# A two-layer trunk on one core: output tiles in the order of tokens' later experts, each step an iteration behind the last, and the last three experts' tokens from rows on chip

## The chip, the cores and the metric

The kernel runs on one core of a Trainium2 chip. The metric is device time in microseconds of one execution; the kernel before is given as the median of three runs. Engine names: PE is TensorE, DVE VectorE, ACT ScalarE, POOL GpSimd, SP SyncE (here only a DMA queue). "L933" is line 933 of the kernel before.

## The reference

A trunk of two layers over 1024 tokens with 16 meta tokens prepended (1040 rows of 1024 numbers). Layer 0 mixes by causal pooling, layer 1 by latent attention; each ends with a mixture of experts, added to the residual. A final root-mean-square norm gives the output, without the meta rows.

```
h = concat(meta_tokens, x)                          # (1040, 1024)
h = h + pool_mixer(rmsnorm(h)); h = h + moe(rmsnorm(h), layer 0)
k, v = shared_latent_kv(h)
h = h + mla_mixer(rmsnorm(h), k, v); h = h + moe(rmsnorm(h), layer 1)
return rmsnorm(h, final_norm)[:, 16:]

def moe(h):                     # 4 groups of 8 experts, D_EXPERT = 256
    g_sel = argmax(softmax(h @ wr_g + br_g)); w_g = max of it
    top_v, top_i = top_k(logits of the group's 8 experts, 2)
    gate = w_g * softmax(top_v)
    for each token and each of its two experts e:
        out[token] += gate * ((silu(x @ w_gate[e]) * (x @ w_up[e])) @ w_down[e])
```

So each token's result is its residual row plus two weighted expert rows, and both of its experts lie in one group of eight.

## The kernel before

Layer 0 runs to about 441 us of the profiled span, the latents and attention to about 975, layer 1's mixture of experts from about 980, the rest of the output after it.

**Routing.** For every token the router (class with `order`, `place_ids`, `lists`) finds its two experts, its rank among the tokens of each, and from these the tables `gi` (which row of h_d each of an expert's up to CAP = 96 places takes), `di` (which row of y_d the result goes to) and the gates. y_d has two halves of L = 1040 rows, one for the first and one for the second expert of a token; h_d holds the residual rows with the normed input. Tokens beyond 96 of an expert go through `overflow` behind the loop, under a branch that does not run with these inputs.

**The expert loop, `Moe.run`.** Iteration e of 33 does, in program order: the gather `ga(e+3)` on GpSimd's DMA queue (L839, 96 rows into one of NX = 6 buffers `xg`); `out.begin(e)`; the down products of expert e-1 and the up products of e on TensorE (L1378 to L1380, three products for each piece split into a high and a low part by ScalarE, L1373, and VectorE, L1374); the transposes of e+1 and their scaling (L860); `rows`, L933, on VectorE, which weighs expert e-1's result and adds the row it was gathered from; `scatter`, L845, 96 rows to y_d; the split of the next x; `out.middle(e)`; the second halves of the products; Silu on ScalarE (L908) and its product on VectorE (L909); `out.end(e)`. The order on every engine is the order of the program. Weights stream through a ring of 17 slots of 1 MB, issued on SP (L827), three a iteration, each waiting for its slot.

**Output under the loop, class `Out`.** Before the change the tokens are put in the order of their expert group: `order` (end of iteration 3) works out each token's place, `place_ids` (L798) writes 128 token numbers to list_d by an indirect DMA, one tile an iteration in iterations 4 to 11, `load_list` (L804) reads the list back on SP in iteration 12, and `lists` makes the row indices. Then `EARLY_OUT` gives tile t an iteration a: in begin(a) both rows of each of its 128 tokens are fetched from y_d (`fetch`, L1097, two gathers of 512 KB), in end(a) VectorE adds them (L1111) and ScalarE squares (L1112), in middle(a+1) VectorE finds the root (L1109, L174 to L184), in end(a+1) it multiplies (L1114), in begin(a+2) the tile is stored (`store`, L1102). Five tiles go this way, in iterations 17, 20, 25, 27 and 29, all through one pair of buffers; `rest` does the other three after the loop, planned by `Sched`. `again`, under a branch, repeats the five if the group order did not suit them.

In dependence tracking an indirect DMA that writes a tensor waits for the one before that wrote it, unless `declare_no_dep` says otherwise; the scatters to y_d are declared apart from one another, the writes of `place_ids` are not. A fetch of y_d waits for the scatters before it, and a scatter behind a fetch waits for the fetch.

## Time and profile before

| | us |
|---|---|
| median of three runs | 1407.7 |
| the runs | 1407.33, 1407.7, 1410.6 |
| the profiled execution's own time | 1410.51 |
| its span | 1408.3 |
| mean granted TensorE clock | 0.954 of full |
| TensorE busy | 1267.9 (90% of the span) |
| VectorE busy | 1054.2 (75%) |
| ScalarE busy | 746.2 (53%) |
| GpSimd busy | 341.4 (24%) |

The median is over whole executions; the profile is of one. The span leaves out 2.2 us of that execution's own time. Busy shares are over the whole span, so they mix stages with different limits.

### The profile page before, as it was taken

The numbers are of one execution on the slowest core, as the hardware profiler recorded it, in microseconds if no ns is written. First come the engines' busy times: TensorE is split into PE (matmuls) and PEld (weight loads), VectorE is DVE, ScalarE is ACT, GpSimd is POOL, SyncE is SP. The second block draws the span as 40 slices with busy tenths as digits, with TensorE's granted clock in tenths as the row PEclk, the third lists the DMA queues.
The fourth block names the chain that finished last, engine by engine and source line by source line (L and its number), as shares of the span: only waits on it lengthen the run. The fifth ranks groups of instructions, "written<-read, shape, count | busy, mean of one in ns | idle before, by whom it ended". The sixth has DMA issues, their size and how long they took to land. (4 is left out here: it accounts for less than half of the span.)

```text
span 1408.3 us, 22733 instructions
## 1 busy us (share of the span) xinstructions
PE 1267.9 (90%) x8027; PEld 1093.4 (78%) x8027; DVE 1054.2 (75%) x2507; ACT 746.2 (53%) x1591; POOL 341.4 (24%) x469
## 2 busy tenths in 40 slices
PE   7979999999995999999999999996999996696870
PEld 5977888888884998989888899985888885585650
DVE  5777888888887676676776777688788885595863
ACT  4445655565655455655655665554556563354440
POOL 0122222222211441232221223213133222122312
PEclk9989999999998999999999999997999998898995
DMA  8927999999945303320010010467899999897213
...
DMA packets 80314, 293.48 MB, mean 208 GB/s; under 512 B 21409, under 2 KB 28833, under 8 KB 63682
## 3 DMA queue, kind: packets, MB, share of 16 engines
...
q8 instruction: 65, 1.06, 0.3%
...
## 5 line engine op out<-in xcount | busy, mean ns | idle before, releaser
L1378 PE MATMUL py<-wp,hT 128*96 128x512 f32 x256 | 115.8, 452 | 43.9 <-ACT hT L1373 43.9
L1378 PE MATMUL gu<-wp,xT 128*96 128x256 f32 x512 | 147.3, 288 | 0.0
L1380 PE MATMUL gu<-wp,xT 128*96 128x256 f32 x512 | 143.4, 280 | 0.0
L1379 PE MATMUL gu<-wp,xT 128*96 128x256 f32 x512 | 143.3, 280 | 0.0
L1374 DVE TENSOR_TENSOR wp<-slotB,wp 128x512 fp32r<-128x512 f32 x160 | 107.0, 690 | 22.5 <-ACT wp L1373 21.6
L1373 ACT ACTIVATE wp<-slotB 128x512 fp32r<-128x512 f32 x160 | 96.0, 626 | 23.8 <-PE py L1380 20.2
L1380 PE MATMUL py<-wp,hT 128*96 128x512 f32 x256 | 104.9, 410 | 1.0 <-DVE hT L1374 0.4
L1379 PE MATMUL py<-wp,hT 128*96 128x512 f32 x256 | 103.7, 405 | 0.0
L2281 POOL TENSOR_TENSOR hh<-hh,wt 128x512 f32<-128x512 f32 x56 | 72.3, 1291 | 111.2 <-ACT wt L2280 109.1
L845 POOL DMA_INDIRECT y_d<-xg,di x34 | 34.2, 1006 | 246.9 <-DVE xg L933 210.7
L1373 ACT ACTIVATE xT<-xq 128x384 fp32r<-128x384 f32 x64 | 33.6, 526 | 111.1 <-DVE xq L860 111.1
L1378 PEld LDWEIGHTS py<-wp,hT 128*96 128x96 f32 x256 | 43.2, 169 | 62.2 <-ACT hT L1373 46.4
L1378 PEld LDWEIGHTS gu<-wp,xT 128*96 128x96 f32 x512 | 84.8, 166 | 0.1
L1380 PEld LDWEIGHTS gu<-wp,xT 128*96 128x96 f32 x512 | 83.1, 162 | 0.0
L1379 PEld LDWEIGHTS gu<-wp,xT 128*96 128x96 f32 x512 | 82.9, 162 | 0.1
L884 PE MATMUL gu<-slotB,xq 128*96 128x256 f32 x320 | 75.6, 379 | 0.0
L2117 ACT ACTIVATE P<-bank,sm 128x400 f32<-128x400 f32 (+3 forms) x112 | 59.6, 540 | 25.7 <-DVE sm L2107 25.5
L1870 DVE TENSOR_TENSOR T<-bank,T 128x512 fp32r<-128x512 f32 (+2 forms) x112 | 53.7, 496 | 20.7 <-ACT T L1866 19.7
L860 DVE TENSOR_TENSOR xq<-pt,ffg 128x768 f32<-128x768 f32 (+1 forms) x66 | 61.0, 927 | 8.1 <-PE pt L857 8.1
L2284 DVE SCALAR_TENSOR_TENSOR hh<-bank,ri,hh 128x512 f32<-128x512 f32 x72 | 53.6, 747 | 15.8 <-PE bank L1380 15.4
L1374 DVE TENSOR_TENSOR wp<-slotR,wp 128x512 fp32r<-128x512 f32 x80 | 53.2, 690 | 13.9 <-ACT wp L1373 13.6
L1374 DVE TENSOR_TENSOR wp<-hh,wp 128x512 fp32r<-128x512 f32 x82 | 54.8, 690 | 11.4 <-ACT wp L1373 10.9
...
## 6 DMA issues: line engine op xcount, KB each, us to landing
...
hh<-w_up SPq DMA_DIRECT2D x10, 1024.0 KB, 10.9
...
```

The lines of the kernel that those rows point to most:

```text
L845: return nc.gpsimd.indirect_dma_start(out=self.r.y_d, out_offset=bass.IndirectOffsetOnAxis(ap=didx, axis=0), in_=y[:CAP], in_offset=None, ...
L860: nc.vector.tensor_tensor(x[:, 4 * a:4 * (a + w)].rearrange("p (a b) c -> p a b c", a=w), pt[:, a:a + w].rearrange("p a (b c) -> p a b c", ...
L884: nc.tensor.matmul(gu[:CAP, f * FE:f * FE + FE], lhsT=x[0][:, j], rhs=w[:, j], start=(f == 0 and j == 0), stop=False)
L1373: nc.scalar.activation(dH, src, AF.Copy)
L1374: nc.vector.tensor_tensor(dL, src, dH.bitcast(F32), op=OP.subtract)
L1378: nc.tensor.matmul(out, lhsT=aH, rhs=bH, start=start, stop=False)
L1379: nc.tensor.matmul(out, lhsT=aH, rhs=bL, start=False, stop=False)
L1380: nc.tensor.matmul(out, lhsT=aL, rhs=bH, start=False, stop=stop)
L1870: nc.vector.tensor_tensor(dL, src, dH.bitcast(F32), op=OP.subtract)
L2117: nc.scalar.activation(self.P[hd, qp][a][:, x0:x0 + xe], tt[:, :xe], AF.Exp, bias=sm[:, 3:4], scale=SCALE, accum_out=sm[:, x:x + 1])
L2281: done(end), s.op("G", end + s.LAT, 1170, lambda: nc.gpsimd.tensor_tensor(k.h[i][:, cs], k.h[i][:, cs], x, op=OP.add), lambda end: s.relea ...
L2284: s.op("V", now + s.LAT, 70 + 1.04 * 512, lambda: nc.vector.scalar_tensor_tensor(k.h[i][:, cs], p, self.ri[hd, i], k.h[i][:, cs], op0=OP.m ...
```

## The change

Tokens are ordered by their later expert (the larger number of the two) instead of by group. `Out` takes over the working; `EARLY_OUT` is now the list of iterations (9, 13, 17, 21, 25, 29, 30) in which seven tiles are fetched.

- The ordering (`order`) is six small steps: `later` in end(0), `masks` in end(1), a pair of matmuls `sums` in begin(2), `starts` in end(2), `places` in end(3), `suits` in end(4). Two operations a batch in the router and one in the counts, which served the group order, go.
- `place_ids` is called four times in begin(4) and four times in begin(5); `load_list` in begin(6); `lists` in end(8). `load_tokens` (begin 6 to 8) gathers the token numbers of the last three experts, `tokens` (end 10) makes indices of them.
- A loaded tile's steps are an iteration apart each: fetch in begin(f); add on GpSimd in begin(f+1), square on ScalarE in middle(f+1), root on VectorE in end(f+1); gain (by the final norm's row) on GpSimd in begin(f+2), scale on ScalarE in middle(f+2); store in begin(f+3). Before, add and gain were VectorE's.
- Tiles 5 and 6 end around the last iterations, and the tokens whose later expert is 29, 30 or 31 (DIRECT = 3) take that expert's rows from the `xg` buffer on chip and fetch only the row of the other expert (`other`). Their store goes by `keep`. `rest` is called inside iteration 32 around the last scatter.
- Fetches and scatters are declared apart from one another (`out.got`), and so are stores.
- In layer 1 the overflow branch stands ahead of the loop, in both layers its room is `xg[5]` instead of `xg[1]`; `again` does all eight tiles through plain loads.
- CLEAR goes from 20000 to 30000, between pieces of the clearing of y_d in the middle stage.

```diff
-EARLY_OUT = ((0, 17, 256), (1, 20, 256), (2, 25, 640), (3, 27, 640), (4, 29, 640))
-LIST_AT = 3
-CLEAR = 20000
-FINAL_START = 2000
+EARLY_OUT = (9, 13, 17, 21, 25, 29, 30)
+DIRECT = 3
+CLEAR = 30000
...
+    def order(self, psum, c):
+        k, V, n = self.k, self.k.nc.vector, len(self.tiles)
+        m = c[1][:, :n * NE].rearrange("p (n e) -> p n e", n=n)
+        q = c[0][:, :n * NE].rearrange("p (n e) -> p n e", n=n)
+        cum = [c[0][:, 512 + NE * i:512 + NE * i + NE] for i in range(2)]
+        st, p, b = c[0][:, 640:640 + NE], c[0][:, 704:704 + n], c[0][:, 720:729]
+        w, tot = c[0][:, :2 * n * NE], c[0][:, 672:672 + NE]
+        pr = psum.tile([128, 2, NE], F32, name="pr", tag="pr", bufs=1)
+        def later():
+            V.tensor_tensor(w.rearrange("p (n e) -> p n e", e=NE), self.oh.rearrange("p n j e -> p (n j) e"),
+                            k.iota32.unsqueeze(1).to_broadcast([128, 2 * n, NE]), op=OP.mult)
+            V.tensor_reduce(self.later.unsqueeze(2), w.rearrange("p (n x) -> p n x", n=n), axis=AX.X, op=OP.max)
+        def masks():
+            V.tensor_tensor(m, k.iota32.unsqueeze(1).to_broadcast([128, n, NE]),
+                            self.later.unsqueeze(2).to_broadcast([128, n, NE]), op=OP.is_equal)
+            V.tensor_reduce(c[0][:, 736:736 + NE].unsqueeze(2), m.rearrange("p n e -> p e n"), axis=AX.X, op=OP.add)
+            V.tensor_copy(self.cnt, c[0][:, 736:736 + NE])
+            V.scalar_tensor_tensor(self.ids, self.v[:, :, 0, 0], float(BIG), self.v[:, :, 0, 1], op0=OP.add, op1=OP.add)
+            V.scalar_tensor_tensor(self.later, self.later, float(BIG), self.ids, op0=OP.mult, op1=OP.add)
+            with k.nc.allow_non_contiguous_dma("one number a row"):
+                for i, t, x in self.runs():
+                    k.nc.sync.dma_start(out=self.later_d[t * 128:(t + x) * 128].rearrange("(t p) o -> p (t o)", p=128),
+                                        in_=self.later[:, i:i + x])
+        def sums():
+            k.nc.tensor.matmul(pr[:, 0], lhsT=k.tri, rhs=self.cnt, start=True, stop=True)
+            k.nc.tensor.matmul(pr[:, 1], lhsT=k.ones, rhs=self.cnt, start=True, stop=True)
+        def starts():
+            a = tot
+            V.tensor_copy(tot, pr[:, 1])
+            for i, n2 in enumerate((1, 2, 4, 8, 16)):
+                x = cum[i % 2]
+                V.tensor_copy(x[:, :n2], a[:, :n2])
+                V.tensor_tensor(x[:, n2:], a[:, n2:], a[:, :NE - n2], op=OP.add)
+                a = x
+            V.tensor_tensor(st, a, tot, op=OP.subtract)
+            V.tensor_tensor(q[:, 0], st, pr[:, 0], op=OP.add)
+        def places():
+            for i in range(n - 1):
+                V.tensor_tensor(q[:, i + 1], q[:, i], m[:, i], op=OP.add)
+            V.tensor_tensor(q, q, m, op=OP.mult)
+            V.tensor_reduce(p.unsqueeze(2), q, axis=AX.X, op=OP.add)
+            V.tensor_copy(self.place, p)
+        def suits():
+            t = len(EARLY_OUT)
+            lim, pos = c[0][:, 768:768 + t], c[0][:, 784:784 + t]
+            for i, e in enumerate(EARLY_OUT):
+                V.tensor_copy(lim[:, i:i + 1], st[:, e - 1:e])
+            V.scalar_tensor_tensor(pos, k.iota32[:, :t], 128.0, self.v[:, 0, 0, 1:2].to_broadcast([128, t]), op0=OP.mult, op1=OP.add)
+            V.tensor_tensor(self.past, pos, lim, op=OP.is_ge)
+            V.scalar_tensor_tensor(b[:, :t - 1], k.iota32[:, 1:t], 128.0, lim[:, :t - 1], op0=OP.mult, op1=OP.is_gt)
+            V.tensor_scalar(b[:, t - 1:t], lim[:, t - 1:], float(128 * t), None, op0=OP.is_gt)
+            V.tensor_reduce(b[:, t:t + 1].unsqueeze(2), self.ex[:, NE - DIRECT:].unsqueeze(1), axis=AX.X, op=OP.add)
+            V.tensor_reduce(b[:, 8:9].unsqueeze(2), b[:, :t + 1].unsqueeze(1), axis=AX.X, op=OP.add)
+            V.tensor_copy(self.bad, b[:, 8:9])
+        return later, masks, sums, starts, places, suits
...
+        V, ids = self.k.nc.vector, self.ids[:, :len(EARLY_OUT)]
+        V.scalar_tensor_tensor(ids, self.past, float(BIG), ids, op0=OP.mult, op1=OP.add)
+        V.tensor_scalar(ids, ids, float(S), None, op0=OP.min)
         for j in range(2):
-            self.k.nc.vector.tensor_scalar(self.list[:, j], self.ids, float(j * L), None, op0=OP.add)
+            V.tensor_scalar(self.list[:, j], self.ids, float(j * L), None, op0=OP.add)
+    def load_tokens(self, i):
+        e = NE - DIRECT + i
+        if i == 0:
+            self.k.nc.vector.memset(self.token, float(NE * BIG))
+        self.k.nc.gpsimd.indirect_dma_start(
+            out=self.token[:CAP, i:i + 1], out_offset=None, in_=self.later_d,
+            in_offset=bass.IndirectOffsetOnAxis(ap=self.gi[:CAP, e:e + 1], axis=0), bounds_check=S - 1, oob_is_err=False)
+    def tokens(self):
+        V = self.k.nc.vector
+        V.scalar_tensor_tensor(self.token, self.k.iota32[:, NE - DIRECT:], -float(BIG), self.token, op0=OP.mult, op1=OP.add)
+        V.tensor_copy(self.ti[:CAP, 0], self.token[:CAP])
+        V.scalar_tensor_tensor(self.token[:CAP], self.token[:CAP], 2.0, self.of[:CAP], op0=OP.mult, op1=OP.subtract)
+        V.tensor_scalar(self.ti[:CAP, 1], self.token[:CAP], float(L), None, op0=OP.add)
...
-            for o in self.scat:
+            for o in self.scat + (out.got if out else []):
...
+        if out:
+            self.overflow(nx, scatter, True)
...
+                if out and e == NE:
+                    out.last()
                 self.rows(ps, r.table[:CAP, 0, e - 1:e], y)
-                scatter(y, r.di[:CAP, e - 1:e])
+                put = lambda y=y, e=e: scatter(y, r.di[:CAP, e - 1:e])
+                if out and e == NE:
+                    out.rest(put)
+                else:
+                    put()
...
-        room = [k.xg[1], 0]
+        room = [k.xg[NX - 1], 0]
+        xg = k.xg[NX - 2]
...
+    def apart(self, x, others):
+        for o in others:
+            self.k.tc.declare_no_dep(x.ins, o.ins, reason="other tokens' rows")
 
     def fetch(self, t, c):
         for j in range(2):
-            self.k.nc.gpsimd.indirect_dma_start(
+            x = self.k.nc.gpsimd.indirect_dma_start(
                 out=c[j], out_offset=None, in_=self.r.y_d, in_offset=bass.IndirectOffsetOnAxis(ap=self.r.list[:, j, t:t + 1], axis=0),
-                bounds_check=2 * L - 1, oob_is_err=True)
+                bounds_check=2 * L - 1, oob_is_err=False)
+            self.got.append(x)
 
     def store(self, t, c):
...
+        self.keep(c, self.r.list[:, 0, t:t + 1])
+    def keep(self, c, ids):
+        n = ids.shape[0]
+        x = self.k.nc.gpsimd.indirect_dma_start(
+            out=self.out[0], out_offset=bass.IndirectOffsetOnAxis(ap=ids, axis=0), in_=c[0][:n], in_offset=None,
+            bounds_check=S - 1, oob_is_err=False)
+        self.apart(x, self.put)
+        self.put.append(x)
+    def other(self, i, o):
+        x = self.k.nc.gpsimd.indirect_dma_start(
+            out=o[:CAP], out_offset=None, in_=self.r.y_d, in_offset=bass.IndirectOffsetOnAxis(ap=self.r.ti[:CAP, 1, i:i + 1], axis=0),
+            bounds_check=2 * L - 1, oob_is_err=False)
+        self.got.append(x)
+    def add(self, eng, c, n=128):
+        eng.tensor_tensor(c[0][:n], c[0][:n], c[1][:n], op=OP.add)
+    def square(self, c, i, n=128):
+        self.k.nc.scalar.activation(c[-1].bitcast(BF16)[:n, :D], c[0][:n], AF.Square, accum_out=self.st[:n, 0, i:i + 1])
+    def root(self, i, n=1):
+        st = self.st[:, :, i:i + n]
+        self.k.nc.vector.tensor_scalar(st[:, 1], st[:, 0], 1.0 / D, EPS, op0=OP.mult, op1=OP.add)
+        for f in rsqrt_ops(self.k, st[:, 2], st[:, 1], st[:, 3]):
+            f()
+    def gain(self, c, n=128):
+        self.k.nc.gpsimd.tensor_tensor(c[0][:n], c[0][:n], self.g[:n], op=OP.mult)
+    def scale(self, c, i, n=128):
+        self.k.nc.scalar.activation(c[0][:n], c[0][:n], AF.Copy, scale=self.st[:n, 2, i:i + 1])
+    def both(self, c, i, n=128):
+        self.k.nc.vector.scalar_tensor_tensor(c[0][:n], c[0][:n], self.st[:n, 2, i:i + 1], self.g[:n], op0=OP.mult, op1=OP.mult)
+    def rows(self, i):
+        x = self.k.xg
+        free = x[(NE - DIRECT) % NX]
+        return [(x[(NE - 4) % NX], self.a[1], self.b[1])[i], x[(NE - DIRECT + i) % NX], self.b[1] if i == 0 else free]
 
 
     def begin(self, e):
-        r = self.r
+        k, r, nc = self.k, self.r, self.k.nc
+        later, masks, sums, starts, places, suits = self.order
+        if e == 2:
+            sums()
         for i in range(len(r.tiles)):
-            if e == LIST_AT + 1 + i:
+            if e == 4 + i // 4:
                 r.place_ids(i)
-        if e == LIST_AT + 1 + len(r.tiles):
+        if e == 6:
             r.load_list()
...
+        if 5 < e < 6 + DIRECT:
+            r.load_tokens(e - 6)
+        for t, f in enumerate(EARLY_OUT[:-2]):
+            if e == f:
+                self.fetch(t, self.a)
+            if e == f + 1:
+                self.add(nc.gpsimd, self.a)
+            if e == f + 2:
+                self.gain(self.a)
+            if e == f + 3:
+                self.store(t, self.a)
+        if e == NE - 3:
+            self.fetch(5, self.a)
+        if e == NE - 2:
+            self.add(nc.gpsimd, self.a)
+            self.fetch(6, self.b)
+            self.other(0, self.rows(0)[0])
+        if e == NE - 1:
+            self.add(nc.gpsimd, self.b)
+            self.add(nc.gpsimd, self.rows(0), CAP)
+            self.other(1, self.rows(1)[0])
+            self.gain(self.a)
+        if e == NE:
+            self.add(nc.gpsimd, self.rows(1), CAP)
+            self.other(2, self.rows(2)[0])
 
     def middle(self, e):
 
-        for t, a, _ in EARLY_OUT:
-            if e == a + 1:
-                for _, _, f in self.steps(self.c, self.st)[2:-1]:
-                    f()
+        for f in EARLY_OUT[:-2]:
+            if e == f + 1:
+                self.square(self.a, 0)
+            if e == f + 2:
+                self.scale(self.a, 0)
+        if e == NE - 2:
+            self.square(self.a, 0)
+        if e == NE - 1:
+            self.square(self.b, 1)
+            self.square(self.rows(0), 2, CAP)
 
     def end(self, e):
...
+        k, r = self.k, self.r
+        later, masks, sums, starts, places, suits = self.order
+        if e == 0:
+            k.nc.vector.memset(self.st, 1.0)
+            k.nc.sync.dma_start(out=self.g, in_=bcast_row(k.A["final_norm"], D))
+            later()
+        if e == 1:
+            masks()
+        if e == 2:
+            starts()
+        if e == 3:
+            places()
+        if e == 4:
+            suits()
+        if e == 8:
             r.lists()
...
+        if e == 10:
+            r.tokens()
+        for f in EARLY_OUT[:-1]:
+            if e == f + 1:
+                self.root(0)
+    def last(self):
+        self.scale(self.a, 0)
+        self.square(self.rows(1), 3, CAP)
+        self.root(1, 3)
+    def rest(self, scatter):
+        nc, V, r = self.k.nc, self.k.nc.vector, self.r
+        b, d = self.b, [self.rows(i) for i in range(DIRECT)]
+        self.store(5, self.a)
+        self.gain(b)
+        scatter()
+        self.gain(d[0], CAP)
+        self.add(V, d[2], CAP)
+        self.scale(b, 1)
+        self.square(d[2], 4, CAP)
+        self.scale(d[0], 2, CAP)
+        self.both(d[1], 3, CAP)
+        self.root(4)
+        self.both(d[2], 4, CAP)
+        self.store(6, b)
+        for i in (1, 0, 2):
+            self.keep(d[i], r.ti[:CAP, 0, i:i + 1])
...
-        self.s.op("Q", now, 0, lambda: self.clear(0, now))
+        self.s.op("Q", now + CLEAR, 0, lambda: self.clear(0, now + CLEAR))
```

## Rows read from the trace of the kernel before

**Rows 1.** Busy time by stretch: length, engines (instructions), granted clock, DMA share, GB/s
```profile
1002.00:1154.00 152.00, 151.60 (x931) 125.89 (x930) 131.09 (x212) 89.85 (x166) 41.94 (x38) 1.00 0.98 328
1154.00:1284.00 130.00, 101.10 (x591) 81.15 (x589) 86.91 (x141) 56.49 (x105) 30.19 (x26) 0.91 0.93 344
1284.00:1370.00 86.00, 67.10 (x360) 50.78 (x360) 63.39 (x111) 40.52 (x76) 20.36 (x17) 0.90 0.31 104
```

**Rows 2.** Waits by engine, 1000 to 1371: total us, times, longest
```profile
DVE out L1111 <- DMA out<-y_d,list: 37.5, 5, 11.4
```

**Rows 3.** Timeline of VectorE in the loop: start, us, instruction [idle before]
```profile
1001.93 1.27 DVE L933 SCALAR_TENSOR_TENSOR xg<-py,table,xg 96x1024 f32<-96x1024 f32 x1
...
1154.15 1.27 DVE L933 SCALAR_TENSOR_TENSOR xgh<-py,table,xgh 96x1024 f32<-96x1024 f32 x1
...
1164.23 1.27 DVE L933 SCALAR_TENSOR_TENSOR hh<-py,table,hh 96x1024 f32<-96x1024 f32 x1
...
1176.96 1.23 DVE L1111 TENSOR_TENSOR out<-out,out 128x1024 f32<-128x1024 f32 x1 [10.20 <-DMA out<-y_d,list]
...
1183.03 0.69 DVE L1374 TENSOR_TENSOR wp<-slotR,wp 128x512 fp32r<-128x512 f32 x1 [0.30 <-ACT wp L1373]
...
1188.21 1.27 DVE L933 SCALAR_TENSOR_TENSOR hh<-py,table,hh 96x1024 f32<-96x1024 f32 x1
...
1189.87 0.14 DVE L1109 TENSOR_SCALAR ost<-ost 128x1 f32<-128x1 f32 x1
...
1191.39 0.16 DVE L184 SCALAR_TENSOR_TENSOR ost<-ost 128x1 f32<-128x1 f32 x1
...
1352.98 1.27 DVE L933 SCALAR_TENSOR_TENSOR hh<-py,table,hh 96x1024 f32<-96x1024 f32 x1
```

**Rows 4.** Timeline behind the loop, all engines
```profile
1370.07 1.28 DVE L933 SCALAR_TENSOR_TENSOR xg<-py,table,xg 96x1024 f32<-96x1024 f32 x1 [1.45 <-PE py L1380]
1371.62 0.91 POOL L845 DMA_INDIRECT y_d<-xg,di  x1 [5.88 <-DVE xg L933]
...
1376.11 1.05 POOL L1097 DMA_INDIRECT c<-y_d,list  x1 [3.58 <-DVE xg L1023]
...
1384.33 1.06 ACT L1112 ACTIVATE c<-c 128x1024 bf16<-128x1024 f32 x1 [16.66 <-DVE c L1111]
...
1399.52 0.96 POOL L1102 DMA_INDIRECT out<-c,list  x1 [3.12 <-issue]
```

**Rows 5.** Timeline at the end of layer 0, all engines
```profile
441.30 0.06 DVE L1023 MEMSET xg<- 128x1 f32 x1 [3.98 <-DMA y_d<-xg,di]
...
442.05 3.28 ACT L1433 ACTIVATE wH<-slotA,gk 128x320 fp32r<-128x320 f32 x7 [8.41 <-DVEq L1029]
```

**Rows 6.** Timeline of GpSimd and VectorE, 478 to 482
```profile
478.57 2.39 POOL L1828 TENSOR_TENSOR hh<-hh,qr 128x1024 f32<-128x1024 f32 x1
...
479.34 1.63 DVE L182 TENSOR_TENSOR st<-st 128x2 f32<-128x2 f32 x1
```

**Rows 7.** Line L798, the writes of the list
```profile
  DMA list_d<-ids,place: 9.7, 6
...
DMA to landing us min/median/max: 8.8/10.1/11.5
```

**Rows 8.** DMA issues of 1000 to 1160: count, KB, median us to landing
```profile
y_d<-xg,di POOLq DMA_INDIRECT x9, 8.4
xg<-h_d,gi POOLq DMA_INDIRECT x9, 10.9
...
ids<-list_d SPq DMA_DIRECT2D x1, 4.0 KB, 25.1
```

**Rows 9.** DMA issues of 1287 to 1409
```profile
y_d<-xg,di POOLq DMA_INDIRECT x5, 3.6
out<-y_d,list POOLq DMA_INDIRECT x4, 4.8
```

**Rows 10.** Timeline of GpSimd in iteration 17, 1160 to 1200
```profile
1164.30 1.05 POOL L1097 DMA_INDIRECT out<-y_d,list  x1 [6.04 <-DMA y_d<-xgh,di]
```

249 lines of the change are left out of this document (101 added, 148 removed).

## The prediction

> **What bounds the kernel now.** I read the busy time of stretches first [rows 1]. From 1002 to 1154 us TensorE is busy for 151.6 of 152 us at full clock: the expert loop runs at TensorE's pace. From 1154 to 1284 it is busy for 101.1 of 130, from 1284 to 1370 for 67.1 of 86. So what this change can win lies in some 48 us of holes in the loop and in the 38.3 us from 1370 to the span's end at 1408.3. It cannot win in the first stretch, only lose there.
>
> The waits name the holes [rows 2]: five adds of output tiles on VectorE waited 37.5 us in all for the fetch of rows of y_d. The VectorE rows show what one costs [rows 3]. An undisturbed iteration takes 10.08 us (1154.15 to 1164.23). The one behind it starts the add at 1176.96, after 10.20 us of waiting, and its own L933 comes at 1188.21, 23.98 us after the last. From 1154.15 (expert 15) to 1352.98 (expert 29) pass 198.83 us where 14 iterations at 10.08 make 141.1: **57.7 us of stalls**, some 14 each for the three tiles fetched while weights still stream, some 8 each for the two after that. From expert 0 to 15 pass 152.22 us, 1.0 over 15 x 10.08: the old ordering work.
>
> Behind the loop [rows 4]: last L933 at 1370.07, its scatter 1371.62, the first of six gathers 1376.11 (held until the scatter landed, 3.58 us of waiting), last store 1399.52. That is 29.45 us from L933 to the last store's issue and 8.8 from there to the span's end.
>
> **What goes.** (1) The five stalls, 57.7 us, and the old ordering, 1.0. (2) The tail of six gathers and three chains. (3) Layer 0's overflow no longer memsets a buffer that the last scatter is still reading. There ScalarE stood 8.41 us until the branch behind that memset, which came at 441.30, after the landing [rows 5]; the buffer of expert 29 is free earlier. Between 0 and 4 us (the landing's wait), I take 2, since the loads of y_d behind it wait for that landing anyway.
>
> **What comes, in order of time.**
>
> *Front.* One branch goes ahead of the loop. From memset to ScalarE's first work behind the branch were 0.75 us [rows 5]; below, nothing, if the wait for the first gather covers it. I take 1. The clearing of y_d, whose pieces the planner of the middle stage now sets 30 us apart instead of 20, I cost at nothing: it lies ahead of its first use in the loop; if it met other transfers there, 0 to 2 us. Two router operations a batch and one in the counts go, about 1 us of a chain of small operations on VectorE of 0.14 us and more [rows 3]. Net 0.
>
> *Ordering, iterations 0 to 4.* The five ends get 3, 5, 13, 10 and 14 VectorE operations, at most two of them in an end 256 or 512 columns wide. At 0.14 to 0.7 us each that is some 1.3 to 2.5 us an iteration, less what an iteration absorbs (the old ordering was 14 operations in one end and cost 1.0): **+4**, between 2 and 7.
>
> *Places.* Before, one indirect write of list_d is issued an iteration; six of the eight begin only when the one before has landed (9.7 us of waiting), and landing takes 10.1 us [rows 7]. They are not declared independent. After the change four stand in GpSimd's queue in iteration 4 and four in iteration 5, behind each other: some 10 us apiece. Queued behind the first four are the scatter of expert 3 and the gather of expert 8, behind the next four the scatter of 4 and the gather of 9. The first place can go at about 1041 (VectorE has the places at the end of iteration 3, whose L933 comes near 1036 with the ordering's delay), landings then at 1051, 1061, 1071: the gather of expert 8 goes near 1073 instead of 1050, lands 10.9 us later [rows 8], and is wanted for the transpose ahead of L933 of expert 6, near 1078 with the ordering's delay: 6 to 8 late. The other four pull the next gather behind by another 4 x 10 if nothing else changes. But SP waits for the last place at its load of the list, now in iteration 6, and issues no weights meanwhile; those under way land within some 25 us, as that load itself did [rows 8]. From about 1080 DMA is then idle, and landings fall to those of the unloaded stretch, 3.6 us [rows 9]. So the last four need some 4 x 3.9 and the second gather comes 5 late on top. **+12**; below, 0 (the waits are covered or not there); above, with loaded landings throughout, some 35 to 45. The weights survive the hold: the ring holds over five experts, and SP stands some 38 us.
>
> *Five tiles under load (iterations 9, 13, 17, 21, 25).* The fetch waits for the last scatter's landing, as now. With T the L933 two experts back, that scatter goes at T+1.5 and lands at T+9.9 [rows 8]; the old tile had its add 12.66 us after its first fetch (1164.30 to 1176.96) [rows 3, 10], so the data are there at T+22.5. The add, now on GpSimd, ends at T+24.9 (2.39 us for 128x1024, [rows 6]). Iteration-behind scheduling asks for the square on ScalarE right behind the split of xT, at T+20.9 (two iterations of 10.08 and some 0.7). So the square still waits 4.0 us, with Silu behind it, and TensorE behind Silu. Its own 1.06 [rows 4] and some 0.2 for reading out the sum go on ScalarE, of which I count 0.9 as free ahead of Silu; the eight root operations at the end of that iteration take 1.7 on VectorE (1189.87 to 1191.55) [rows 3] ahead of the next splits. Later the gain on GpSimd holds VectorE. The row: while GpSimd adds from 478.57 for 2.39 us, a 128x2 operation of VectorE takes 1.63 us [rows 6], where a small one takes 0.14 to 0.16 [rows 3]; in the loop each L1374 split, 0.69 [rows 3], has both inputs in SBUF and would be held too. About 1 more. Sum 4.0 + 0.3 + 1.7 + 1.0 = 7 a tile against 14 now, 4 for the first, where the places leave the DMA emptier: **+32**. Below, 0 to 2 a tile (fetch landing two us sooner and the square covered), so +8; above, 10 a tile, so +50. The two late tiles left holes like these, and in their stretch the granted clock was 0.90, so between 2.4 and 1.2 GHz [rows 1]; a tenth of the 67.1 us busy there is 6.7 us for three holes, part of it in idle time. So 0 to 2 a tile, I take **+2.5** in all.
>
> The Trainium skill, SBUF — State Buffer, section Who interferes with whom, says that a VectorE instruction with two SBUF inputs contends with a GpSimd one that reads SBUF, and that whichever issued first blocks the other. The trace agrees for VectorE being held (1.63 against 0.16). No row shows GpSimd held by VectorE; by the rule the 14 GpSimd operations of the change could each lose time too, which would speak against it and is priced as a rival.
>
> *Iterations 29 to 31.* Two adds of tiles, one of 96 rows and two gains on GpSimd, two tile squares and one of 96 rows on ScalarE. Each 2.4 us holds splits, each square holds Silu: from the same sums +1.5, +3.5 and +3: **+8**.
>
> *End.* In iteration 32: add of expert 30's rows, 2.4, then the last fetch; scale, square, three roots. From the last L933: gain of tile 6 at once, 2.4; scatter; gain of 96 rows to about 7.4, held behind VectorE's add and both (1.3 each); scale of tile 6 and of the rows 1.06 each, square 1.25, root 1.7, last both 1.3 until about 9.9; four stores at 1.0 to 1.4 each from 7.4 on. Last store issued at about **11.5** behind L933 instead of 29.45 [rows 4]: **-18**, between -12 and -20. What follows it stays 8.8, perhaps 1 less as no branch code for more gathers stands there: **-1**.
>
> **Sum.** -57.7 - 1.0 + 4 + 12 + 32 + 2.5 + 8 = -0.2 in the loop; I leave it at 0. Then -18, -1, layer 0 -2: together about **-21**; I round to -22, as the last branch and its code also leave. From the profiled 1410.5 (span 1408.3 and 2.2 around it) that is 1388.5; the profiled run is 2.8 over the median 1407.7, so **1386** as a median. In words: the loop gives back nearly all that the stalls cost, and the tail is the gain.
>
> **Rivals.**
> *Covered* (chance 0.17). The places don't hold the gathers, or the squares find the tile there. Speaks for it: in the unloaded stretch fetches land in 4.8 us [rows 9]; against it: 10.1 for a place under load [rows 7]. Then places cost 0 to 4, tiles 2 to 3 each: 20 to 30 us less, about 1362.
> *Ends on the other side: eight places in a row at loaded landings* (0.13). Point of decision: whether DMA empties while SP is held. If landings stay at 10 us, eight last until 1125, the gathers of experts 8 and 9 come some 45 late instead of 12, and weights come short after it: +33 to +40 over the forecast, about 1422. Against it: SP is the only source of the heavy traffic.
> *Shared port dear, tail half as good* (0.20). GpSimd operations are themselves held by VectorE's splits (0.69 each) or take 3 us or more, tiles cost 9 to 10 and iterations 29 to 31 15: +12 to +20, about 1400, reaching into no change. The skill's rule above is its mechanism.
> *Does not do what it says*: list out of order so the repair behind the loop runs. Then some 8 tiles more, over 60 us slower; 0.01, since with the reference's inputs no expert has more than 85 tokens where 96 fit, and the seven limits of the order (295, 344, 536, 596, 779, 830, 863) reach the ends that they must (128, 256, ... 768 for the first six), the last staying under 896; it is not in the range.
> The forecast itself has 0.49, its own range 1376 to 1397.
>
> **Range and chances.** All but 2 in 10: 1360 to 1413, which leaves out the places' case and the far end of Covered. A change under 0.3% (4.2 us) cannot be told from none. Faster by more (under 1403.5): forecast, Covered and most of the shared-port case, 0.78. Within: 0.08. Slower (over 1411.9): 0.14.
>
> **What would show it.** L933 from 1001.93 on: delays in iterations 6 to 8 of some 12 us in sum, with GpSimd rows of L798's successor waiting for list_d and a thinned DMA share near 1080; iterations 10, 14, 18, 22, 26 near 17 us with ScalarE waiting at the square for GpSimd's add; VectorE splits of over 0.69 us while GpSimd adds; last store 11 to 12 us behind the last L933. It goes wrong most easily at the places (both ways) and at whether the square waits 0 or 6 us.

## The result and the profile after

The changed kernel takes 1392.0 us (median of four runs, 1389.0 to 1392.6) against 1408.3 (four runs, 1407.3 to 1410.6): a ratio of 0.9878, 95% interval 0.9859 to 0.9897, so 14.5 to 19.9 us faster. The forecast was 1386, range 1360 to 1413. The profiled execution of after is the fastest of its four (span 1387.2), the one of before the slowest of its four (span 1408.3); their spans differ by 21.1 us, and the terms below are taken from these two.

The start of an expert's `rows` (L933 before, L999 after, same operation) cuts both spans into pieces; "iteration n" below is the time from the rows of expert n-1 to those of n. "Places" are the eight writes of the list by `place_ids`. From the rows of VectorE:

| us | before | after | difference |
|---|---|---|---|
| start of expert 0's rows | 1001.93 | 1000.48 | -1.5 |
| expert 0 to 9 | 91.68 | 96.54 | +4.9 |
| expert 9 to 28 | 242.99 | 233.90 | -9.1 |
| expert 28 to 31 | 33.47 | 38.56 | +5.1 |
| expert 31 to the end | 38.23 | 17.72 | -20.5 |
| span | 1408.30 | 1387.20 | -21.1 |

Inside the loop, expert 0 to 31, the two differ by 0.9 us: what the five stalls [rows 3] cost has come back in other places. What remains is mostly the tail. [rows 4] show it before, this timeline of GpSimd behind the loop shows it after (last rows at 1369.48):

```profile
1371.04 1.87 POOL L911 DMA_INDIRECT y_d<-xg,di  x1 [3.10 <-DVE xg L999]
...
1375.62 1.00 POOL L1197 DMA_INDIRECT out<-xg,list  x1 [0.16 <-issue]
...
1380.20 0.91 POOL L1197 DMA_INDIRECT out<-xgh,ti  x1 [0.31 <-issue]
```

The last store goes 10.72 us behind the rows instead of 29.45, and nothing waits for the scatter's landing any more. No run undoes a part of the tail's change, so what the new order, the rows on chip and the missing gathers are worth each is not shown.

Where the loop lost time again, by stretch (columns as in [rows 1]: length, busy time of PE, PEld, DVE, ACT and POOL, granted clock, DMA share, GB/s):

```profile
1000.00:1097.00 97.00, 92.64 (x566) 75.97 (x565) 84.62 (x165) 54.41 (x100) 35.26 (x31) 1.00 0.89 298
1097.00:1154.00 57.00, 47.53 (x270) 38.02 (x268) 40.78 (x67) 26.34 (x48) 17.81 (x14) 0.91 0.99 374
1154.00:1284.00 130.00, 116.29 (x672) 93.45 (x671) 104.33 (x166) 71.11 (x130) 45.83 (x36) 0.95 0.92 341
...
1341.40:1369.50 28.10, 18.91 (x80) 12.41 (x78) 26.59 (x40) 13.89 (x26) 18.07 (x11) 0.82 0.25 78
```

The first stretch, where before TensorE had no hole, now has 4.4 us of them; the first tile's stretch 9.5 of 57; the last iterations 9.2 of 28.1, at a granted clock of 0.82. The waits of the squares in 1100 to 1345, with one of them, and then those of the places (line L844, before [rows 7]):

```profile
ACT out L1215 <- POOL out L1212: 25.1, 5, 8.4
```

```profile
1154.96 1.06 ACT L1215 ACTIVATE out<-out 128x1024 bf16<-128x1024 f32 x1 [3.33 <-POOL out L1212]
```

```profile
  DMA list_d<-ids,place: 22.0, 7
...
DMA to landing us min/median/max: 2.1/3.8/6.8
```

The five squares waited 25.1 us for GpSimd's adds; before, five adds waited 37.5 us for the fetches [rows 2]. The wait has moved from the add to the square. VectorE's rows of the loop follow: the first tile's iteration, then the second tile's with one operation of its root, then the last three experts.

```profile
1097.02 1.27 DVE L999 SCALAR_TENSOR_TENSOR xgh<-py,table,xgh 96x1024 f32<-96x1024 f32 x1
...
1120.34 1.27 DVE L999 SCALAR_TENSOR_TENSOR hh<-py,table,hh 96x1024 f32<-96x1024 f32 x1
...
1150.98 1.27 DVE L999 SCALAR_TENSOR_TENSOR xg<-py,table,xg 96x1024 f32<-96x1024 f32 x1
...
1157.26 2.46 DVE L179 SCALAR_TENSOR_TENSOR ost<-ost 128x1 f32<-128x1 f32 x1
...
1167.08 1.27 DVE L999 SCALAR_TENSOR_TENSOR xg<-py,table,xg 96x1024 f32<-96x1024 f32 x1
```

```profile
1341.38 1.27 DVE L999 SCALAR_TENSOR_TENSOR hh<-py,table,hh 96x1024 f32<-96x1024 f32 x1
...
1347.53 3.43 DVE L1554 TENSOR_TENSOR wp<-kr,wp 128x512 fp32r<-128x512 f32 x2
...
1351.15 3.62 DVE L1554 TENSOR_TENSOR wp<-kr,wp 128x512 fp32r<-128x512 f32 x2
...
1357.11 1.27 DVE L999 SCALAR_TENSOR_TENSOR xg<-py,table,xg 96x1024 f32<-96x1024 f32 x1
...
1364.96 3.02 DVE L181 TENSOR_TENSOR ost<-ost 128x3 f32<-128x3 f32 x1
...
1369.48 1.28 DVE L999 SCALAR_TENSOR_TENSOR xg<-py,table,xg 96x1024 f32<-96x1024 f32 x1
```

The iteration of the first tile's square takes 23.32 us, the next one's 16.10 (18, 22 and 26 take 17.33, 18.05 and 17.51). L179 at 1157.26 takes 2.46 us where such an operation takes 0.22. At the end a pair of splits takes 3.43 and 3.62 us instead of 1.28, and a root operation 3.02 instead of 0.16. GpSimd's rows at those times:

```profile
1152.15 2.77 POOL L1212 TENSOR_TENSOR out<-out,out 128x1024 f32<-128x1024 f32 x1 [7.14 <-DMA out<-y_d,list]
...
1157.34 2.36 POOL L1224 TENSOR_TENSOR out<-out,out 128x1024 f32<-128x1024 f32 x1
```

The gain at 1157.34 stands on top of the root at 1157.26. What is held there are operations with two inputs in SBUF: under the last gain (first line) a one-input operation takes its usual 0.15 us, the two-input one behind it 1.76 instead of 0.22.

```profile
1372.93 2.53 POOL L1224 TENSOR_TENSOR hh<-hh,out 96x1024 f32<-96x1024 f32 x1
```

```profile
1373.54 0.15 DVE L173 TENSOR_SCALAR ost<-ost 128x1 int32<-128x1 int32 x1
1373.73 1.76 DVE L179 SCALAR_TENSOR_TENSOR ost<-ost 128x1 f32<-128x1 f32 x1
```

### The profile page after: what moved, and what is told of

It reads as the page before. It is cut to its first block, busy times and chain, and to the rows that moved or that the text cites. A ratio compares the mean times of both kernels' runs of the same rounds, so it can differ in the third digit from the quotient of the medians.

```text
span 1387.2 us, 22810 instructions
## 1 busy us (share of the span) xinstructions
PE 1279.1 (92%) x8029; PEld 1100.5 (79%) x8029; DVE 1071.8 (77%) x2529; ACT 756.4 (55%) x1603; POOL 391.1 (28%) x492
## 5 line engine op out<-in xcount | busy, mean ns | idle before, releaser
L975 DVE SCALAR_TENSOR_TENSOR hm<-gu,table,hm 96x256 f32<-96x256 f32 x64 | 30.7, 480 | 49.3 <-ACT hm L974 49.3
L1559 PEld LDWEIGHTS py<-wp,hT 128*96 128x96 f32 x256 | 42.7, 167 | 30.8 <-DVE wp L1554 13.7
L1560 PEld LDWEIGHTS py<-wp,hT 128*96 128x96 f32 x256 | 42.7, 167 | 27.1 <-DVE hT L1554 9.4
```

The lines of the kernel that those rows point to most:

```text
L1559: nc.tensor.matmul(out, lhsT=aH, rhs=bL, start=False, stop=False)
L1560: nc.tensor.matmul(out, lhsT=aL, rhs=bH, start=False, stop=stop)
```

## The experiments

Each run, cut into the pieces of the table above; "over" is the time from expert 9 to 28 less 191.6 us, which is 19 undisturbed iterations as run e1 has them. All columns behind the median are of one execution. Iteration 1, inside "0 to 9", has the same code in after and in every run but e10, and took 12.6 us in five of them and 14.3 in seven: TensorE waits 2.26 us in it, and the granted clock of 1005 to 1010 was then 1.00 in after and 0.79 in e11. So 1.7 us there say nothing of an edit.

| run | median us (runs) | span | rows of expert 0 | 0 to 9 | 9 to 28, over | 28 to 31 | to the end |
|---|---|---|---|---|---|---|---|
| before | 1408.3 (4) | 1408.3 | 1001.9 | 91.7 | 51.4 | 33.5 | 38.2 |
| after | 1392.0 (4) | 1387.2 | 1000.5 | 96.5 | 42.3 | 38.6 | 17.7 |
| e1 no tiles | 1348.3 (1) | 1346.4 | 999.3 | 98.5 | 0.0 | 40.4 | 16.6 |
| e2 tiles' DMA alone | 1357.2 (1) | 1355.2 | 1000.2 | 97.6 | 5.3 | 43.2 | 17.3 |
| e12 no gain | 1381.7 (1) | 1379.9 | 997.0 | 99.6 | 31.8 | 42.3 | 17.6 |
| e4 behind Silu | 1395.5 (1) | 1393.7 | 999.5 | 99.0 | 44.3 | 41.6 | 17.6 |
| e3 list on GpSimd's queue | 1396.4 (1) | 1394.6 | 1000.4 | 113.7 | 32.7 | 38.6 | 17.7 |
| e5 places apart | 1389.0 (4) | 1384.0 | 998.1 | 95.4 | 39.5 | 41.6 | 17.8 |
| e9 room back | 1399.7 (4) | 1400.5 | 1006.4 | 98.4 | 46.3 | 40.0 | 17.7 |
| e6 tiles on VectorE | 1358.1 (4) | 1353.8 | 998.6 | 95.9 | 12.1 | 38.0 | 17.6 |
| e11 add on GpSimd, rest as e6 | 1357.9 (4) | 1357.0 | 999.6 | 97.8 | 11.8 | 38.6 | 17.6 |
| e7 end on VectorE | 1387.3 (4) | 1385.0 | 998.1 | 98.3 | 46.6 | 36.7 | 13.7 |
| e8 e6 and e7 | 1357.3 (4) | 1351.5 | 996.3 | 95.4 | 11.6 | 43.2 | 13.4 |
| e10 e8 and four edits more | 1347.2 (5) | 1345.6 | 999.8 | 93.8 | 6.4 | 40.5 | 13.4 |

The ratios to the kernel before: e5 0.9848 (0.9832 to 0.9865), e6 0.9637 (0.9619 to 0.9656), e7 0.9829 (0.9812 to 0.9845), e8 0.9629 (0.9604 to 0.9655), e9 0.9923 (0.9899 to 0.9946), e10 0.9551 (0.9536 to 0.9566), e11 0.9634 (0.9615 to 0.9653).

**What a tile costs.** e1 drops the five tiles:

```diff
         for t, f in enumerate(EARLY_OUT[:-2]):
-            if e == f:
-                self.fetch(t, self.a)
-            if e == f + 1:
-                self.add(nc.gpsimd, self.a)
-            if e == f + 2:
-                self.gain(self.a)
-            if e == f + 3:
-                self.store(t, self.a)
+            pass
...
-        for f in EARLY_OUT[:-2]:
-            if e == f + 1:
-                self.square(self.a, 0)
-            if e == f + 2:
-                self.scale(self.a, 0)
...
-        for f in EARLY_OUT[:-1]:
-            if e == f + 1:
-                self.root(0)
+        if e == EARLY_OUT[-2] + 1:
+            self.root(0)
```

> Leaves out the five tiles of iterations 9 to 25 altogether (fetch, add, square, root, gain, scale, store), so five eighths of the output stay unwritten. In the changed kernel the iterations 10, 14, 18, 22 and 26 took 23.32, 16.10, 17.34, 18.05 and 17.51 us instead of 10.08, and the iterations behind them a little more, together some 42 us. Both theories expect all of that gone: these iterations at 10.1 us, span 1387.2 - 42 = about 1345 us. If the first of them stays at over 13 us, its delay comes from the weights' catching up after the hold and not from the tile.

All of it went: 0.0 over, and iteration 10 took 10.09 us. So the 42.3 us are the tiles', the first one's 13 included. e2 keeps their transfers (square, scale and root go as in e1):

```diff
             if e == f:
                 self.fetch(t, self.a)
-            if e == f + 1:
-                self.add(nc.gpsimd, self.a)
-            if e == f + 2:
-                self.gain(self.a)
             if e == f + 3:
                 self.store(t, self.a)
...
```

> Keeps the five tiles' fetches and stores and leaves out their add, square, root, gain and scale, so these tiles are stored unsummed and unscaled. Theory (a tile costs because ScalarE waits for GpSimd's add, and because GpSimd holds VectorE): as without the tiles, iterations at 10.1 to 11 us, span about 1345 to 1352 us. Rival (a tile costs because 1 MB of gathered rows and 0.5 MB of stores delay weights and gathers): iterations 10 to 26 stay long, span 1375 to 1390 us.

5.3 us over, so the transfers are not the cost in the changed kernel. The span, 1355.2, is still 3.2 above the theory's bound, as iteration 30 took 20.77 us (15.73 in after). TensorE by stretch in this run:

```profile
1108.00:1249.00 141.00, 141.00 (x868) 117.55 (x867) 120.89 (x182) 83.12 (x154) 44.51 (x39) 1.00 1.00 365
1249.00:1300.00 51.00, 46.94 (x282) 38.33 (x281) 39.55 (x61) 27.16 (x51) 14.44 (x13) 1.00 0.93 350
```

TensorE is busy for all of the first 141 us with the DMA share at 1.00; only behind 1249 do weights come short, by 4.1 us. In e6, e8, e10 and e11, which have the tiles' transfers too and small stalls left, TensorE waits for no weights.

**Wait, order or hold.** e4 changes the order alone:

```diff
     def middle(self, e):
...
-            if e == f + 1:
-                self.square(self.a, 0)
             if e == f + 2:
-                self.scale(self.a, 0)
+                self.root(0)
...
     def end(self, e):
...
             if e == f + 1:
-                self.root(0)
+                self.square(self.a, 0)
+            if e == f + 2:
+                self.scale(self.a, 0)
```

> Only the order changes, nothing is left out: for the five tiles square and scale go behind Silu instead of ahead of it, and the root into the middle of the next iteration. Theory (what costs is that Silu, and with it TensorE, stands behind a square that waits 3.3 to 8.4 us): the wait now falls on ScalarE's splits for the next down products, of which some 2 us are covered, and the root's 1.7 to 4 us leave the end of the iteration: iterations 14 to 26 at 12.5 to 14.5 us instead of 16.1 to 18, span about 1368 us (1362 to 1375). Rival (the load on GpSimd and DMA counts, not the order): no change, 1384 to 1391 us.

This missed: 44.3 over, no better. The five squares' iterations fell by 4.6 us together, and those behind them, with the root and the scale in them, rose by 6.6. VectorE, then GpSimd, in that run at the third tile:

```profile
1201.25 0.48 DVE L975 SCALAR_TENSOR_TENSOR hm<-gu,table,hm 96x256 f32<-96x256 f32 x1 [0.31 <-ACT hm L974]
1204.88 4.20 DVE L1556 TENSOR_TENSOR wp<-qr,wp 128x512 fp32r<-128x512 f32 x2 [3.15 <-ACT wp L1555]
1209.01 0.34 DVE L1556 TENSOR_TENSOR hT<-ph,hT 128x192 fp32r<-128x192 f32 x1
1209.28 1.28 DVE L1556 TENSOR_TENSOR wp<-qr,wp 128x512 fp32r<-128x512 f32 x2
```

```profile
1200.40 2.75 POOL L1212 TENSOR_TENSOR out<-out,out 128x1024 f32<-128x1024 f32 x1 [6.56 <-DMA out<-y_d,list]
...
1205.57 2.36 POOL L1224 TENSOR_TENSOR out<-out,out 128x1024 f32<-128x1024 f32 x1
```

The square still stands 1.96 us in ScalarE's queue, now with the splits of the next down products behind it; and the gain, at 1205.57, falls on VectorE's splits, two of which take 4.20 us instead of 1.28. Half an iteration was not late enough, and the gain's hold was not in the theory. e12 takes the gain away:

```diff
-            if e == f + 2:
-                self.gain(self.a)
```

> The changed kernel without GpSimd's gain for the five tiles of iterations 9 to 25 (the final norm's row is left out of these tiles); add, square, root, scale, stores as they were. In the changed kernel the square waited 8.4, 3.3, 3.3, 5.3 and 4.7 us, and one root operation took 2.46 us instead of 0.22 while the gain ran. Theory (the tile's 6 to 8 us are the square's wait plus what the gain holds): the 2.2 us go from each of the five iterations, 16.1, 17.3, 18.1 and 17.5 become 14 to 15.8, span about 1376 us. Rival (the wait alone sets the iteration, the root is covered by it): the iterations stay within 0.7 us, span 1385 to 1389.

31.8 over, 10.5 less. That bears the theory out in sum, but not tile by tile: iteration 14 rose to 17.70, its square waiting 5.1 us instead of 3.3, and the span lies between what theory and rival gave. The squares' waits differ from run to run, so I take them off: the iterations of the five squares are 13.2, 6.0, 7.3, 8.0 and 7.4 us over 10.08 in after, of which the squares waited 8.4, 3.3, 3.3, 5.3 and 4.7, which leaves 16.8; in e12 10.7, 7.6, 4.7, 5.0 and 3.8, less 8.1, 5.1, 3.3, 3.9 and 3.3, which leaves 8.0. If each us of waiting lengthens the iteration by one, which no run shows by itself, the gain's hold is (16.8 - 8.0) / 5, some 1.8 us a tile; the wait is 5.0 on average; the square itself, the root and the lower clock are the other 1.6.

e6 gives the sum the time that it needs, and puts both tile operations back on VectorE:

```diff
                 wp = self.up_pieces(e)
+            if out:
+                out.early(e)
...
     def begin(self, e):
...
-            if e == f + 1:
-                self.add(nc.gpsimd, self.a)
-            if e == f + 2:
-                self.gain(self.a)
...
+    def early(self, e):
+        for f in EARLY_OUT[:-2]:
+            if e == f + 2:
+                self.square(self.a, 0)
     def middle(self, e):
         for f in EARLY_OUT[:-2]:
-            if e == f + 1:
-                self.square(self.a, 0)
             if e == f + 2:
-                self.scale(self.a, 0)
+                self.root(0)
...
     def end(self, e):
...
+            if e == f + 1:
+                self.add(k.nc.vector, self.a)
+            if e == f + 2:
+                self.both(self.a, 0)
```

> The five tiles of iterations 9 to 25 with VectorE's operations in place of GpSimd's, and later: add on VectorE at the end of iteration f+1, square on ScalarE behind the splits of the up pieces of f+2, root in the middle of f+2, gain and scale as one VectorE operation at the end of f+2, store in f+3. Nothing is left out. Theory (a tile costs because its square asks for the sum half an iteration too early, and because GpSimd's add and gain hold VectorE's splits and small operations for 2 to 3 us each): 1 to 3 us a tile instead of 6 to 8, the first 5 to 8 instead of 13; weights come short by some 5 us around iterations 25 to 28, as without the tiles' arithmetic; span 1360 to 1370 us. Rival (VectorE, busy 86% of an iteration, has no room for 4.2 us a tile, as before the change): 5 us and more a tile, span 1376 to 1388 us.

1358.1 us, 34 less than after, and better than the theory: the span is below its 1360 to 1370, and the 5 us of missing weights that it counts did not show. VectorE at the third tile, and the square on ScalarE:

```profile
1185.69 1.23 DVE L1214 TENSOR_TENSOR out<-out,out 128x1024 f32<-128x1024 f32 x1
...
1196.94 1.27 DVE L1233 SCALAR_TENSOR_TENSOR out<-out,ost,out 128x1024 f32<-128x1024 f32 x1
...
1204.47 1.27 DVE L999 SCALAR_TENSOR_TENSOR xg<-py,table,xg 96x1024 f32<-96x1024 f32 x1
```

```profile
1183.32 0.53 ACT L1559 ACTIVATE xT<-xq 128x384 fp32r<-128x384 f32 x1 [1.62 <-DVE xq L926]
...
1191.69 1.04 ACT L1217 ACTIVATE out<-out 128x1024 bf16<-128x1024 f32 x1
...
1193.41 0.53 ACT L1559 ACTIVATE xT<-xq 128x384 fp32r<-128x384 f32 x1 [0.59 <-DVE xq L926]
```

The add starts with no wait behind hm, the square lies in ScalarE's idle time ahead of xT (idle before xT falls from 1.62 to 0.59), and what is left is 1.1 us in iteration f+2, where `both` stands ahead of the splits. The first tile still took 16.00. e11 tells whether the engine of the add matters:

```diff
     def begin(self, e):
...
+            if e == f + 1:
+                self.add(nc.gpsimd, self.a)
...
     def end(self, e):
...
-            if e == f + 1:
-                self.add(k.nc.vector, self.a)
```

> As the run with VectorE's tiles (span 1353.8 us, 1.1 us a tile and 5.9 for the first), but the add is on GpSimd in the next iteration, as in the changed kernel; square, root and the joined gain and scale stay late. Nothing is left out. Theory (the early square and the gain's hold of VectorE are the cost; the add alone falls where VectorE has but few splits): 1 to 3 us a tile, span 1353 to 1362 us. Rival (any GpSimd pass over a tile costs its 2 to 3 us on VectorE): 3 to 4.5 us a tile, span 1363 to 1372 us.

The same time as e6 (1357.9). From e12 to e11 the 31.8 over fall to 11.8: between them lie the later square, the later root and the joining of gain and scale on VectorE, which no run separates. The add holds splits here too, yet costs about 1 us of iteration f+1 (11.12 us at the second tile):

```profile
1145.07 3.52 DVE L1560 TENSOR_TENSOR wp<-slot,wp 128x512 fp32r<-128x512 f32 x2 [0.16 <-ACT wp L1559]
```

In sum the engine of the add is worth little, but for two effects that cancel: GpSimd's add costs about 1 us at each later tile, and the first tile's iteration is 12.02 us instead of 16.00, since its late rows hold up GpSimd and not VectorE, which in e6 waits 4.1 us for them. What counts is when the sum is asked for, and what stands under the gain.

**The list's places.** e3 reads the list back on another queue, so SP streams on:

```diff
-            self.k.nc.sync.dma_start(out=self.ids, in_=self.list_d...
+            self.k.nc.gpsimd.dma_start(out=self.ids, in_=self.list_d...
```

> The list is read back on GpSimd's queue instead of SP's, so SP is not held while the places land, and weights go on streaming. Theory (the hold empties the DMA and so makes the places cheap; the weights' catching up makes the first tile dear): places land in 8 to 11 us each instead of 2.1 to 6.8, the gathers of experts 8 and 9 come late, iterations 5 to 8 grow by 20 to 35 us together; the first tile's iteration falls from 23.3 to 16 to 18 us; span 1387.2 + 15 to + 30. Rival (the places are cheap whatever SP does): iterations 5 to 8 unchanged within 3 us, only the first tile cheaper, span about 1381 us.

Expert 0 to 9 took 113.7 us, 17 more than in after (1.7 of it iteration 1), and the first tile's iteration 14.70 instead of 23.32. The places waited for each other for 34.9 us instead of 22.0, and TensorE for a gather behind them:

```profile
  DMA list_d<-ids,place: 34.9, 7
```

```profile
1087.43 1.52 PE L923 MATMUL pt<-cb,xgh 96*128 96x96 f32 x8 [11.46 <-DMA xgh<-h_d,gi]
```

Iterations 5 to 9 grew by 15.5 us, not by 20 to 35, as the places mostly began 6 to 9 us apart; the span, 7.4 over that of after, falls short of the theory's 15 to 30 as well. The theory's direction holds: SP's hold makes the places cheap, and part of what it defers is paid at the first tile. e5 lets the places go without waiting for each other:

```diff
+        for o in self.placed:
+            self.k.tc.declare_no_dep(x.ins, o.ins, reason="other places")
```

> Only change: the eight writes of the list are declared apart from one another, so they no longer wait for each other's landing. Theory (in the changed kernel the row of places costs little itself, some 1 us in iterations 7 and 8, but holds SP for 14 us, and the weights that catch up afterwards make the first tile's iteration 23.3 us long): the hold gets shorter, iterations 7 and 8 at 10.1 to 10.5 us, the first tile's iteration falls to 16 to 19 us, span 1380 to 1384 us. Rival (the first tile is late for the queue of gathers and scatters on GpSimd alone): that iteration stays over 21 us, span 1385 to 1388 us.

SP waited 5.7 us for the places instead of 19.6, and the DMA share of 1050 to 1060 was 0.94 instead of 0.44. Iterations 7 and 8 came at 10.09 and 10.08, the first tile's at 19.36, just over the bound: of the 6 us by which the first tile is dearer than the others in after, 4 go with the hold. 1389.0 us against 1392.0, with ratio intervals that overlap: the direction is as expected, its size within what these runs tell.

**Layer 0.** e9 undoes the room:

```diff
-        room = [k.xg[NX - 1], 0]
+        room = [k.xg[NX - 1 if first else 1], 0]
```

> Undoes one part of the change: layer 0's overflow code works in the buffer of expert 31 again, as before the change, so its first memset waits for the last scatter. In the changed kernel TensorE's first products behind layer 0 started at 440.38 us, before at 444.48. Theory (2 us of that survive, the rest is given back since the rows of y_d are loaded behind the same scatter): these products at 444 to 445 us, the first expert's rows of layer 1 some 1 to 3 us later than in the changed kernel, the whole +2 us. Rival (nothing survives, the middle stage has its own bounds): same time within 1 us. Rival (all of it survives): +4 us.

1399.7 us against 1392.0. Timelines of the end of layer 0, after first, then e9 (before in [rows 5]):

```profile
437.67 0.06 DVE L1099 MEMSET hh<- 128x1 f32 x1
437.96 3.73 ACT L1613 ACTIVATE wH<-slotA,gk 128x320 fp32r<-128x320 f32 x8 [5.33 <-DVEq L1105]
...
440.38 5.13 PE L1698 MATMUL bank<-wH 128*128 128x320 f32 x24 [3.98 <-ACT wH L1613]
```

```profile
442.51 0.06 DVE L1099 MEMSET xg<- 128x1 f32 x1 [3.97 <-DMA y_d<-xg,di]
...
443.26 3.73 ACT L1613 ACTIVATE wH<-slotA,gk 128x320 fp32r<-128x320 f32 x8 [9.96 <-DVEq L1105]
...
445.69 1.70 PE L1698 MATMUL bank<-wH 128*128 128x320 f32 x5 [8.47 <-ACT wH L1613]
```

The memset waits for the landing again, TensorE starts 5.3 us later and expert 0's rows 5.9 later. Of both, 0.8 stood ahead of the edit: the last rows of layer 0 start at 437.26 in e9 and at 436.44 in after. So the room is worth 4.5 us there and 5.1 at expert 0; all of it survives, which was the second rival. The spans differ by 13.3 us; the other 7.4 lie in the loop, where the edit has no part: 1.7 in iteration 1, the rest mostly in tiles' iterations.

**The end, and both.** e7 puts the last two tiles and the direct rows on VectorE, their squares behind the up pieces and their stores in begin(31) and begin(32):

```diff
     def end(self, e):
...
+        if e == NE - 3:
+            self.add(k.nc.vector, self.a)
+        if e == NE - 2:
+            self.both(self.a, 0)
+            self.add(k.nc.vector, self.b)
+            self.add(k.nc.vector, self.rows(0), CAP)
+        if e == NE - 1:
+            self.both(self.b, 1)
+            self.both(self.rows(0), 2, CAP)
+            self.add(k.nc.vector, self.rows(1), CAP)
...
     def rest(self, scatter):
...
         scatter()
-        self.gain(d[0], CAP)
         self.add(V, d[2], CAP)
-        self.scale(b, 1)
         self.square(d[2], 4, CAP)
-        self.scale(d[0], 2, CAP)
         self.both(d[1], 3, CAP)
...
```

> The five tiles as in the changed kernel; the last two tiles and the tokens of the last three experts with VectorE's operations in place of GpSimd's: adds at the ends of iterations 29, 30 and 31, gain and scale as one operation. Nothing is left out. Theory (in iterations 29 to 31 GpSimd's adds and gains hold VectorE for 2 to 3 us each): iteration 30 falls from 15.7 to 11 to 12.5 us, iteration 31 from 12.4 to 8 to 10, the last store goes 7 to 9 us behind the last expert's rows instead of 10.7; span 1374 to 1379 us. Rival (the work costs the same on either engine, as VectorE has 6 us more of it): within 4 us of 1387.

The tail fell by 4.0 us, as expected, and iteration 30 from 15.73 to 12.58, just over the bound; iteration 31 missed and rose to 13.35, as root, two `both` and an add now stand ahead of its splits. From expert 28 to the end that saves 5.9 us; the tiles, which the edit does not touch, took 4.3 more in this execution. Span 1385.0, within what the rival gave; the median, 1387.3, is 4.7 below that of after, with ratio intervals apart.

> The two edits of the tiles and of the end together, nothing left out. If their gains add up, span 1347 to 1360 us; if the weights' stream is the next limit, the stalls move to waits for slots in iterations 20 to 28, and the span stays above 1358.

1357.3, no better than e6 (the span, 1351.5, lies where the gains add up, but two of the four runs took 1360.5): the tail's 4 us were lost in iteration 29, 17.66 us long, where the add, no longer an iteration behind its fetch, waits for it:

```profile
1303.51 1.23 DVE L1214 TENSOR_TENSOR out<-out,out 128x1024 f32<-128x1024 f32 x1 [6.09 <-DMA out<-y_d,list]
```

e10 moves that fetch and all the others but the last an iteration earlier, and mends the ordering; its places are declared apart as in e5:

```diff
-EARLY_OUT = (9, 13, 17, 21, 25, 29, 30)
+EARLY_OUT = (8, 12, 16, 20, 24, 28, 30)
...
     def begin(self, e):
...
-        if e == 2:
-            sums()
...
-        if e == NE - 3:
+        if e == NE - 4:
             self.fetch(5, self.a)
...
     def middle(self, e):
+        if e == 2:
+            self.order[2]()
...
-        if e == 8:
+        if e == 7:
             r.lists()
```

> The tiles' and the end's VectorE operations together with: places declared apart, the counting products of the ordering in the middle of iteration 2 instead of its start (TensorE waited 2.26 us there for VectorE's counts), all tiles but the last one iteration earlier (fetches in 8, 12, 16, 20, 24, 28 and 30), lists ready at the end of iteration 7. Nothing is left out. Against the two edits together (span 1351.5): iteration 1 falls by 2, the first tile's iteration from 15.8 to 11 to 13, iteration 29 from 17.7 to 11 to 12. If that is all, span 1335 to 1341 us; if the weights' stream is the next limit, TensorE waits for slots in iterations 22 to 29 and the span is 1341 to 1348.

1347.2 us, a ratio of 0.9551, the fastest of all. Iteration 1 fell to 10.27, the first tile's (9) to 10.23 with 11.84 behind it, iteration 29 to 10.25; no waits of TensorE for weights appeared. The wait moved to iteration 30, 17.03 us, where the last tile's add, at 1309.14, comes right behind the landing of its second fetch, issued at 1302.71 (TensorE idle for 4.14 us), so the span is 1345.6 and not 1335 to 1341.

## Why the prediction came out as it did

**Tail, -18 and -1: right.** Measured -18.7 to the last store and -1.8 behind it, read from the two timelines alone.

**Four loaded tiles at 7: right, in size and in cause.** Iterations 14, 18, 22 and 26 are 28.7 us over, where 28 stood. The square's wait was 3.3 to 5.3 (4.0 stood), the gain's hold 1.8 as worked out from e12 (1.0 stood). The 2.5 for the clock is inside these iterations: the granted clock of 1097 to 1284 was 0.91 and 0.95.

**The first tile, 4, and the places, 12: both mis-sized, and that their sum came out is luck.** The places cost 1.2 us (iterations 5 to 9) and the first tile 13.2 (0.4 more behind it): 14.8 where 16 stood. For the places, the step that failed is "some 10 us apiece": the first four landed in 6.8, 5.7, 6.2 and 4.9 us, three of them while the DMA share was still 1.00 (1040 to 1050), so the gather of expert 8 was in time; why they landed sooner than the 10.1 of before stays open. The last four landed in 2.1 to 2.6 us (3.9 stood). The times of that sum are also an iteration late: in iteration 3 stand the rows of expert 2, at 1023.97, so the first place went at 1029.35 and not at 1041, and DMA was thin from 1050 to 1070 and not from 1080. For the first tile the step that failed is "where the places leave the DMA emptier", since the share is 1.01 from 1070 on:

```profile
1050.00:1060.00 10.00, 10.00 (x63) 8.37 (x62) 8.57 (x14) 5.84 (x12) 5.32 (x6) 1.00 0.44 152
...
1070.00:1080.00 10.00, 9.09 (x57) 7.37 (x56) 7.53 (x15) 5.01 (x9) 5.10 (x5) 1.00 1.01 350
```

The weights catch up, and the first tile's add starts 12.3 us behind the issue of its second fetch (1091.40 to 1103.74; 10.8 at the second tile), with a scatter 2 us late ahead of both: its square waited 8.4. e3 shows both halves at once, e5 the second: without the thin DMA the first tile costs 9.3, close to the 6.9 to 8.3 of the other four in that run.

**Ordering, +4: right in size (4.7 in iterations 1 to 4), but not all from VectorE's row.** TensorE waited 2.26 us for the counts at the start of iteration 2; e10, with the products later, has iteration 1 at 10.27.

**Iterations 29 to 31, +8: 11.6 measured** (over 10.08 twice and the 6.79 us that iteration 31 took before). The mechanism is as stated, splits held to 3.4 and 3.6 us, but three GpSimd passes fall on VectorE's work in iteration 30. The last tile's gain, which the prediction put behind the last rows, ran ahead of them at 1365.55 and held the three roots there (the 3.02 us above).

**Layer 0, -2, and the front, 0.** Undone, the room costs some 5 us (e9); in after TensorE's first products come 4.1 us earlier, not 2. It is partly paid back: from the router's rank products (at 974.18 before, 971.28 after) to expert 0's rows after takes 29.20 us and before 27.75, with TensorE waiting 1.80 us behind the new branch, where 1 was set against savings of 1. Another 1.2 us are lost between layer 0 and the rank products. Their cause stays open; the pieces of the clearing of y_d, now 30 us apart, lie there, and no run puts them back.

**The rivals.** Of Covered, half came true: the places cost 1.2 us, within its 0 to 4, but the squares did not find the sum there. Places at loaded landings did not come true; e3 has the condition that was named, SP not held, and iterations 5 to 9 grew by 15.5 us, less than half of the 33 to 40 over the forecast that stood. The shared port did not come true at its price of 9 to 10 us a tile: the four loaded tiles cost 7.2 each. Its mechanism did. The rule of the Trainium skill (SBUF — State Buffer, Who interferes with whom), that a VectorE instruction with two SBUF inputs contends with a GpSimd one that reads SBUF, says what the rows of after, e4 and e11 above show. GpSimd is held too, but less: its pass, 2.33 to 2.40 us otherwise, took 2.77 at 1152.15, up to 2.92 elsewhere in after and 2.93 in e11.

**Size.** The spans moved by 21.1 us, 22 stood; the medians moved by 16.3, as the profiled executions were the two ends of their sets. The step from the profiled run to the median was where the forecast lost 6 us. Inside the loop 58.5 us stood for what comes and 59.8 came: the places and the tiles were 3 us cheaper together than forecast with the clock's 2.5, iterations 29 to 31 3.6 dearer and the ordering 0.7.
